# Griffin-style block on one core: the second tile's token roots reach rows by way of DRAM instead of TensorE

## The chip, the cores and the metric

The kernel runs on one core of a Trainium2 chip. The metric is the device time of one execution in microseconds (us), as the median of three timed runs. Beside these runs one execution was recorded by the hardware profiler; all rows of a profile below come from that one.

The engines are named as the profile names them: PE is TensorE with its matmuls, PEld its weight loads, DVE is VectorE, ACT is ScalarE, POOL is GpSimd and SP is SyncE. POOL and SP issue most DMAs here, each into a queue of its own; both queues run on the same 16 DMA engines.

## The reference

One layer over 2048 tokens of width 1024, in float32. The part that bears on this change is the first norm, whose inverse root per token scales all that follows:

```python
def rms_norm(x, g):
    xf = x.astype(jnp.float32)
    y = xf * lax.rsqrt(jnp.mean(xf * xf, axis=-1, keepdims=True) + EPS)
    return (y * g.astype(jnp.float32)).astype(x.dtype)

def hybrid_layer(x, norm_g, w_in, ...):
    h = rms_norm(x, norm_g)
    u = jnp.einsum('bsd,dc->bsc', h, w_in)
    v_c, b_c, c_c, z_c, q, k, v, z_a, gate_logits = jnp.split(u, SPLIT_POINTS, axis=-1)
    y_c = b_c * causal_depthwise_conv(c_c * v_c, conv_w) * jax.nn.silu(z_c)
    y_a = jnp.einsum('bsc,cd->bsd', y_c, w_conv_out)
    q, k = rms_norm(heads(q), q_norm_g), rms_norm(heads(k), k_norm_g)
    o = sliding_window_attention(q, k, heads(v), sinks) * jax.nn.silu(z_a)
    y_b = jnp.einsum('bsc,cd->bsd', o, w_attn_out)
    g_a, g_b = jnp.split(jax.nn.sigmoid(gate_logits + gate_b), N_BRANCHES, axis=-1)
    return x + jnp.einsum('bsd,de->bse', g_a * y_a + g_b * y_b, w_out)
```

(`heads` stands for the reshape into heads of 64. The attention looks back over 128 positions.)

## The kernel before

**Tiling.** The tokens are worked in two tiles of 1024 (`T`), called t = 0 and t = 1. Within a tile, q is the half of 512 tokens (`H`). Activations stand with channels on the 128 rows (partitions) and tokens along them, so that PE can take them as the moving operand. Each matmul in float32 is made of three in the fast 32-bit form, from a high and a low part of each operand, and the products of a 2 x 2 block of outputs are made in seven parts instead of eight, from sums of operands (`sunit`, L493; its products run in line L480). A unit like `cv0` or `z1` is one such block. `SEQ0` and `SEQ1` give the units of the two tiles in order.

**What sets the order.** The order is written out by hand and not by a scheduler. PE runs through the units; after each product, `run` goes on by one tick, prepares a piece of the next weights, calls the functions that `put(n, f)` has set down for that tick, and lets DVE do some steps of woven chains. So everything that is not a product hangs on a tick number, and each engine and each DMA queue takes its instructions in the order in which they were called.

**The attention** of tile t runs inside the same units, in 32 pieces (head group j, block b). A piece `3_7` has these steps: scores on PE (L1027), exponentials on ACT, a turn of 32 x 32 blocks on DVE, a way out to DRAM and back (`fd`, then `x`, both on POOL's queue: L1071, L1078), copies `xh` and `yp` on ACT, the low part `xl` on DVE, four selects on POOL (L1099), then the values matmuls `po` on PE (L1116), whose result goes to DRAM by a write on SP and an adding write `od` on POOL (L1132).

**The roots of tile 1.** The sum of squares of a token is taken with tokens on the rows, so the root of each token stands on its row: a column of 128 values for each block of 128 tokens. While tile 0's gate units run, `h_stats` loads the eight blocks of tile 1 (`x_0` to `x_7`, on POOL's queue, L1372), squares them on ACT, makes the inverse roots on DVE in small steps on 128 x 2 (`x_rsqrt`, `hr`), and keeps them in `rt[q]`, one tile of 128 x 4 for each half q.

To scale activations that have channels on the rows, the 512 roots of a half must stand along each row, the same in all 128 rows. That is done by `h_prep`, which starts with unit `z0` of tile 0: `roots(q)` calls `x_roots`, which has PE turn each root column, spread over 128 columns, into a bank (four matmuls against `ident` for each half, L614, in two banks `ptr` that are borrowed from the attention's scores), and has ACT copy the bank to `rb[q]` (L616).

Then, for four pairs of channel chunks j, `ld` loads `h` (L1418, POOL's queue, four loads for each j), `norm` scales it on DVE by `rb[q]` and writes three of four to DRAM (`hd`, L1425), and sums of the four are written as well (`sdh`). The first pair follows three ticks into `z0`, right behind the roots, the others at ticks 15, 28 and 80 (`H_AT`). In tile 0 the roots are turned by the same `x_roots`; this stays.

**Names in the z units.** `Xz`, `Vz` and `Y` are the three banks of a unit; `wz_...` are its weights in high, low and sum forms; `zin` is what is gated and `zs` the gate. `Vz<-s5z,Y` is an add on DVE that reads `Y` before PE goes on to write it. `th` is the same kind of step in a gate unit.

**Slots.** Tiles of 128 x 512 come from one pool of 19 slots (`slot`), and a tile whose slot was in use waits for those who used it.

Of the kernel before, what the change touches and what calls it, by code (L numbers as in the profile page):

```python
# [8 lines left out]
F32 = mybir.dt.float32  # L9
# [6 lines left out]
P = 128  # L16
# [3 lines left out]
H = 512  # L20
HB = H // P
NB = T // P
# [83 lines left out]
def block_kernel(  # L106
# [12 lines left out]
    nc = tc.nc  # L119
    S = x.shape[1]  # L120
    NT = S // T
# [12 lines left out]
    ps_s = ctx.enter_context(tc.tile_pool(name="ps_s", bufs=1, space=bass.MemoryType.PSUM))  # L134
    ps_m = ctx.enter_context(tc.tile_pool(name="ps_m", bufs=3, space=bass.MemoryType.PSUM))
    dram = ctx.enter_context(tc.tile_pool(name="dram", bufs=1, space=bass.MemoryType.DRAM))

    def slot(shape, dt, name):
        return big.tile(shape, dt, tag="big", name=name)
# [7 lines left out]
    def mbank(name):  # L147
        return ps_m.tile([P, HB, P], F32, tag="m", name=name)
# [14 lines left out]
    ocd = [dram.tile([KC, P, T], F32, name=f"ocd{t}") for t in range(NT)]  # L163
    ycd = [dram.tile([KC, P, T], F32, name=f"ycd{t}") for t in range(NT)]
    hd = [None] + [dram.tile([KC, P, T], F32, name=f"hd{t}") for t in range(1, NT)]
    sd = {}
    for key in [(k, t) for t in range(NT) for k in "hca"][1:] + [("w", 0)]:
        sd[key] = dram.tile([4, KP, P, H], F32, name="sd" + "_".join(str(i) for i in key))
# [4 lines left out]
    def hs(q):  # L173
        return slice(q * H, (q + 1) * H)
# [426 lines left out]
    def x_square(xt, ss, i, junk=None):  # L601

        nc.scalar.activation(out=xt if junk is None else junk, in_=xt, func=AF.Square, accum_out=ss[:, i : i + 1])

    def x_rsqrt(t, b0, n, ss, dst, root=False):
        ms = small.tile([P, n], F32, tag="sm", name=f"ms{t}_{b0}")
        return rsqrt(ms, n, f"hr{t}_{b0}", ss, 1.0 / D, lambda r: nc.vector.tensor_copy(dst, r), root)

    def x_roots(t, q, rs, pt=None):

        if pt is None:
            pt = mbank(f"ptr{t}_{q}")
        for b in range(HB):
            nc.tensor.transpose(pt[:, b, :], rs[:, b : b + 1].to_broadcast([P, P]), ident)  # L614
        rb = slot([P, H], F32, f"rb{t}_{q}")
        nc.scalar.copy(rb, pt.rearrange("p b q -> p (b q)"))  # L616
        return rb
# [4 lines left out]
    def x_norm(h, c, rb):  # L622
        vec.scalar_tensor_tensor(
            out=h, in0=h, scalar=gain(c), in1=rb, op0=ALU.mult, op1=ALU.mult)
# [53 lines left out]
    def put(n, f):  # L678
        at.setdefault(max(n, tick[0] + 1), []).append(f)
# [524 lines left out]
    def sums_of(key, j, r, eng, n0=None):  # L1204

        def first():
            sub(r[0, 0], r[0, 1], r[0, 0])
            eng.dma_start(sd[key][0, j], r[0, 0])
            sub(r[0, 1], r[1, 1], r[0, 1])
            eng.dma_start(sd[key][2, j], r[0, 1])  # L1210

        def second():
            sub(r[1, 1], r[1, 1], r[0, 0])
            eng.dma_start(sd[key][1, j], r[1, 1])
            sub(r[1, 0], r[1, 0], r[1, 1])
            eng.dma_start(sd[key][3, j], r[1, 0])

        if n0 is not None:
            put(n0, first)
            put(n0 + 1, second)  # L1220
        return second, first
# [142 lines left out]
    def h_stats(t, n0):  # L1364

        st = x_state(t)
        xs, rt, seen_ = st["x"], {}, {}

        def ld(b):
            xs[b] = upool.tile([P, 2 * H + 2], F32, tag="u", name=f"x{t}_{b}")[:, 0:D]  # L1370
            r0 = t * T + b * P
            nc.gpsimd.dma_start(xs[b], x2[r0 : r0 + P, :])  # L1372

        def square(b):
            if b % 2 == 0:
                st["ss"][b] = small.tile([P, 2], F32, tag="sx", bufs=3, name=f"ss{t}_{b}")
            x_square(xs[b], st["ss"][b - b % 2], b % 2)

        def norm(b0):
            q, i = divmod(b0, HB)  # L1380
            if i == 0:
                rt[q] = small.tile([P, HB], F32, tag="sr", bufs=2, name=f"rt{t}_{q}")
            seen_[b0] = x_rsqrt(t, b0, 2, st["ss"][b0], rt[q][:, i : i + 2])

        for b in range(NB):
            put(n0 + 2 * b, lambda b=b: ld(b))
            put(n0 + 2 * b + 3, lambda b=b: square(b))
            if b % 2:
                put(n0 + 2 * b + 4, lambda b=b: norm(b - 1))
                put(n0 + 2 * b + 6, lambda b=b: seen_[b - 1]())  # L1390
        st["rt"] = rt

    def h_prep(t, n0):

        st = x_state(t)
        rb = {}

        def roots(q):
            if q == 0:
                rb["banks"] = ps_s.tile([P, 2, HB, P], F32, tag="s", name=f"ptr{t}")  # L1400
            rb[q] = x_roots(t, q, st["rt"][q], rb["banks"][:, q])

        for q in range(2):
            put(n0 + H_AT[0] + q, lambda q=q: roots(q))
        for j in range(KP):
            r = {}

            def ld(q, j=j, r=r):
                if j < H_UP and q == 0:
                    for p in range(2):  # L1410
                        two = upool.tile([P, 2 * H + 2], F32, tag="u", name=f"h{t}_{2 * j + p}")
                        for k in range(2):
                            r[p, k] = two[:, hs(k)]
                for p in range(2):
                    if j >= H_UP:
                        r[p, q] = slot([P, H], F32, f"h{t}_{q}_{2 * j + p}")
                    c = 2 * j + p
                    nc.gpsimd.dma_start(  # L1418
                        r[p, q], xt2[c * P : (c + 1) * P, t * T + q * H : t * T + (q + 1) * H])

            def norm(q, j=j, r=r):
                for p in range(2):
                    x_norm(r[p, q], 2 * j + p, rb[q])
                    if (p, q) != (0, 1):
                        nc.gpsimd.dma_start(hd[t][2 * j + p, :, hs(q)], r[p, q])  # L1425

            n = n0 + 1 + H_AT[j]
            for q in range(2):
                put(n + q, lambda q=q, f=ld: f(q))
                put(n + q + 3, lambda q=q, f=norm: f(q))  # L1430
            sums_of(("h", t), j, r, nc.gpsimd, n + 7)
# [35 lines left out]
    for n in range(S // P // 2):  # L1467
        t, c0 = divmod(2 * n * P, T)
# [7 lines left out]
    def x_state(t):  # L1476
        return state.setdefault(t, {"raw": {}, "ops": {}, "x": {}, "ss": {}})
# [3 lines left out]
    st = x_state(0)  # L1481
# [177 lines left out]
    for t in range(NT):  # L1659
# [29 lines left out]
        if t + 1 < NT:  # L1689
            h_stats(t + 1, tick[0] + STATS_AT)  # L1690
# [76 lines left out]
```

## Time and profile before

| | us |
|---|---|
| median of three runs | 1890.16 |
| lowest and highest of them | 1889.24, 1890.19 |
| the profiled execution | 1888.86 |
| its span, first to last instruction | 1887.1 |

| where it is | from the span's start, us |
|---|---|
| `rt` written by DVE (four copies) | 420.9 to 463.5 |
| `ptr` turned on PE, tile 1 | 575.0 to 578.5 |
| `h` scaled on DVE (sixteen steps) | 589.0 to 807.9 |

How to read the profile: a row of a timeline gives the start, the duration, the engine, the line of the kernel, the operation, its output and inputs by the program's names without buffer numbers, shapes, and a count where equal instructions follow one another. Square brackets at its end give how long the engine had stood idle before and what it waited for. Rows of waits give who waited for whom, the total, the number of times and the longest. A row of windows gives the stretch, the busy time of PE, PEld, DVE, ACT and POOL with instruction counts, the granted clock of PE, the share of time that the DMA engines were busy, and the GB/s they moved. The granted clock of PE is 1.000 over the whole run.

### The profile page before, as it was taken

What the parts mean: (1) busy time and instruction counts of PE and PEld (TensorE: products, weight loads), DVE (VectorE), ACT (ScalarE), POOL (GpSimd) and SP (SyncE); (2) the same over time, 40 slices, a digit from 0 to 9 for tenths busy, and PEclk for the clock granted to TensorE, in tenths of its full rate; (3) what the DMA queues carried; (4) which work ended last, traced back from release to release, by engine and by line L of the source; (5) the groups of instructions that cost most, each with busy time, mean ns of one, the idle gap of its engine ahead of it and who ended that gap; (6) DMA issues with size and microseconds to landing.
All of it is one profiled execution on the core that took longest, in us unless ns stands there. A gap on an engine that the chain in (4) does not pass through costs nothing.

```text
span 1887.1 us, 27889 instructions
## 1 busy us (share of the span) xinstructions
PE 1879.4 (100%) x8638; PEld 1565.4 (83%) x8638; DVE 1539.9 (82%) x2536; ACT 989.2 (52%) x1993; POOL 728.3 (39%) x1038
## 2 busy tenths in 40 slices
PE   9999999999999999999999999999999999999999
PEld 7888888888888888888887888888888888888887
DVE  7989888789878889887579988988888779887654
ACT  7665554567665345435455645556566436344321
POOL 1472454556767111021075445656666211121000
PEclk9999999999999999999999999999999999999999
DMA  8475566689989978899367667768888869999653
GB/s 307 130 212 174 141 176 191 182 252 294 253 244 261 319 272 296 290 288 290 112 186 219 183 169 206 208 166 238 248 237 259 269 244 342 321 281 274 222 173 110
DMA packets 261188, 435.81 MB, mean 231 GB/s; under 512 B 33648, under 2 KB 124784, under 8 KB 261040
## 3 DMA queue, kind: packets, MB, share of 16 engines
q1 hardware_dynamic: 202848, 314.13, 50.6%
q0 software_dynamic: 58048, 119.87, 24.2%
q8 instruction: 69, 1.13, 0.3%
q14 instruction: 79, 0.65, 0.1%
q10 hardware_dynamic: 144, 0.03, 0.0%
HBM read 279.48 MB, written 154.42 MB: 230 GB/s over the span
## 4 chain that ended last, share of the span: by engine, by line
PE 84%; issue 5%; DVE 5%; DMA 3%; POOL 1%; ACT 1%; SPq 0%; POOLq 0%; DVEq 0%; ACTq 0%
PE Y L480 30%; PE Vcv L480 5%; PE Xcv L480 5%; PE s L1027 3%; PE Xz L480 2%; PE Xb L480 2%; PE Vb L480 2%; PE Vz L480 2%; PE Xza L480 2%; PE Xo L480 2%; PE Vo L480 2%; PE Vza L480 2%; PE po L1116 2%; PE Vyb L480 2%; PE Xyb L480 2%
## 5 line engine op out<-in xcount | busy, mean ns | idle before, releaser
L1078 POOL DMA_DIRECT2D x<-fd x256 | 144.2, 612 | 73.1 <-DMA fd<-f 42.9
L1099 POOL TENSOR_SCALAR_AFFINE_SELECT xh<-xh 64x512 fp32r<-64x512 f32 x64 | 67.4, 1053 | 130.2 <-DVE xl L262 95.7
L1051 ACT ACTIVATE p<-s,st,rq 128x128 f32<-128x128 f32 x256 | 113.1, 451 | 7.4 <-DMA lows<-kd 3.3
L1071 POOL DMA_DIRECT2D fd<-f x64 | 39.2, 613 | 176.3 <-DVE f L262 156.8
L480 PE MATMUL Xcv<-oph,wcv_ah 128*128 128x512 f32 x256 | 79.1, 390 | 0.0
L1132 POOL DMA_DIRECT2D od<-o x64 | 69.4, 1091 | 24.1 <-DMA od<-o 9.1
L855 POOL DMA_DIRECT2D q2d<-q_h x64 | 44.4, 693 | 82.7 <-ACT q_h L850 81.7
L1322 POOL DMA_DIRECT2D md<-thyb x32 | 27.5, 874 | 101.7 <-DVE thyb L262 88.8
L1099 POOL TENSOR_SCALAR_AFFINE_SELECT xl<-xl 64x512 fp32r<-64x512 f32 x64 | 62.5, 976 | 4.4
L1099 POOL TENSOR_SCALAR_AFFINE_SELECT yp<-xl 64x512 fp32r<-64x512 f32 x64 | 56.6, 885 | 3.1
L1099 POOL TENSOR_SCALAR_AFFINE_SELECT yp<-yp 64x512 fp32r<-64x512 f32 x64 | 54.8, 856 | 4.2
L480 PEld LDWEIGHTS Xcv<-oph,wcv_ah 128*128 128x128 f32 x256 | 47.6, 188 | 9.4
L262 DVE SCALAR_TENSOR_TENSOR y<-u,cols,y 128x512 f32<-128x512 f32 x64 | 51.5, 805 | 3.7 <-ACT y L1161 2.5
L262 DVE TENSOR_TENSOR opa<-ina,opa 128x512 fp32r<-128x512 f32 x56 | 36.2, 687 | 18.8 <-ACT opa L297 18.8
L262 DVE TENSOR_TENSOR p<-p,st 128x512 f32<-128x512 f32 x64 | 49.2, 769 | 2.8
L1051 ACT ACTIVATION_READ_ACCUMULATOR p<-s,st,rq 128x1 f32 x256 | 50.8, 198 | 0.0
L362 ACT CAST wcv_sh<-wcv_raw 128x1024 fp32r<-128x1024 f32 x16 | 16.9, 1054 | 63.9 <-DVE wcv_raw L262 63.9
L480 PE MATMUL Xcv<-oph,wcv_al 128*128 128x512 f32 x128 | 49.9, 390 | 0.0
L855 POOL DMA_DIRECT2D q2d<-q_l x64 | 44.2, 691 | 14.2 <-DVE q_l L262 10.0
L262 DVE TENSOR_TENSOR opc<-inc,opc 128x512 fp32r<-128x512 f32 x56 | 36.1, 686 | 14.4 <-ACT opc L297 14.2
L262 DVE STREAM_TRANSPOSE f<-p 128x512 f32<-128x512 f32 x64 | 45.4, 710 | 2.6 <-DVE p L262 0.2
L480 PE MATMUL Y<-oph,wcv_d 128*128 128x512 f32 x192 | 46.4, 390 | 0.0
(793 smaller groups left out, 6596.6 us busy)
## 6 DMA issues: line engine op xcount, KB each, us to landing
wcv_raw<-in_w_in SPq DMA_DIRECT2D x32, 512.0 KB, 4.1
q<-q2d SPq DMA_DIRECT2D x64, 256.0 KB, 4.7
v<-vd SPq DMA_DIRECT2D x128, 128.0 KB, 4.4
fd<-f POOLq DMA_DIRECT2D x64, 256.0 KB, 3.8
x<-fd POOLq DMA_DIRECT2D x256, 64.0 KB, 3.4
gd<-th SPq DMA_DIRECT2D x64, 256.0 KB, 3.5
wq_raw<-in_w_in SPq DMA_DIRECT2D x16, 512.0 KB, 5.1
q2d<-q_h POOLq DMA_DIRECT2D x64, 128.0 KB, 3.8
```

Of the source, the lines that this page charges most:

```text
L262: r = f(*args, **kw)
L362: return (lambda: nc.scalar.copy(hi, src), lambda: vec.tensor_tensor(out=lo, in0=src, in1=hi.bitcast(F32), op=ALU.subtract))
L480: nc.tensor.matmul(ps, lhsT=w[:, j, :], rhs=b[:, m, :], start=start and j == 0 and i == 0, stop=j == KP - 1 and i == 2, skip_group_check=n ...
L855: nc.gpsimd.dma_start(q2d[t][j][half, q * 2 * HB : (q + 1) * 2 * HB, i, e, :], src[HALVES[e]].bitcast(F32).rearrange("p (b x) -> p b x", x ...
L1027: nc.tensor.matmul(to, lhsT=w, rhs=x_, start=n == 0, stop=n == 2, skip_group_check=h == 1)
L1051: nc.scalar.activation(out=p[:, i, :], in_=sg[:, i, HD : 3 * HD], func=AF.Exp, bias=st[:, 1, i : i + 1], scale=rv[:, i // 2, i % 2 : i % 2 ...
L1071: nc.gpsimd.dma_start(fd, f)
L1078: nc.gpsimd.dma_start(x[QUADS[k]], src[k])
L1099: nc.gpsimd.affine_select(out=d4, in_=s4, pattern=[[0, 2], [-32 * sg, 2], [0, G], [-sg, 32]], compare_op=ALU.is_gt if prev else ALU.is_ge, ...
L1116: nc.tensor.matmul(po[:, cs], lhsT=v2[:, kind, :], rhs=xx[:, :, h * HD : (h + 1) * HD], start=h == 0 and n == 0, stop=n == 2, skip_group_c ...
L1132: put(tick[0] + ADD_WAIT, lambda: nc.gpsimd.dma_start(to, o[UH].rearrange("p c e q -> p (c e) q"), accum_op=ALU.add))
L1322: nc.gpsimd.dma_start(md[t][k, :, hs(q)], m, accum_op=ALU.add)
```

## The change

The roots of tile 1 take another way from `rt[q]` to `rb[q]`. `h_stats` writes each half's 128 x 4 roots to a DRAM buffer `rxd`, in the order block, token, so that 512 roots stand in a row; `roots(q)` in `h_prep` then loads that row into all 128 rows of `rb[q]`. Both DMAs are issued on POOL. The turns on PE, the bank pair `ptr` and ACT's two copies are no longer called for tile 1. Nothing else is edited.

```diff
     hd = [None] + [dram.tile([KC, P, T], F32, name=f"hd{t}") for t in range(1, NT)]
+    rxd = [None] + [dram.tile([NB, P], F32, name=f"rxd{t}") for t in range(1, NT)]
...
                 put(n0 + 2 * b + 6, lambda b=b: seen_[b - 1]())
-        st["rt"] = rt
+        for q in range(2):
+            put(n0 + 2 * (q + 1) * HB + 6, lambda q=q: nc.gpsimd.dma_start(
+                rxd[t][q * HB : (q + 1) * HB].rearrange("b r -> r b"), rt[q]))
...
         def roots(q):
-            if q == 0:
-                rb["banks"] = ps_s.tile([P, 2, HB, P], F32, tag="s", name=f"ptr{t}")
-            rb[q] = x_roots(t, q, st["rt"][q], rb["banks"][:, q])
+            rb[q] = slot([P, H], F32, f"rb{t}_{q}")
+            src = rxd[t][q * HB : (q + 1) * HB].rearrange("b r -> (b r)")
+            nc.gpsimd.dma_start(rb[q], src.unsqueeze(0).to_broadcast([P, H]))
```

How the instructions stand. The numbers at the end of names are the program's buffer numbers, which shift by a few from one kernel to the other, as line numbers do.

PE, around the second four turns, between the products 1 and 7 of unit `z0`, before:

```order
L480 MATMUL Xz_0_6198<-oph_2_3_533,wz_0_ah 128x512 x2
L480 MATMUL Xz_0_6198<-oph_2_3_533,wz_0_al 128x512
L614 MATMUL ptr_6284<-ident,rt_1_4717 128x128 x4
L480 MATMUL Y<-oph_7_0_910,wz_0_th 128x512 x2
L480 MATMUL Y<-oph_7_0_910,wz_0_tl 128x512
```

and now:

```order
L481 MATMUL Xz_0_6201<-oph_2_3_534,wz_0_ah 128x512 x2
L481 MATMUL Xz_0_6201<-oph_2_3_534,wz_0_al 128x512
L481 MATMUL Y<-oph_7_0_911,wz_0_th 128x512 x2
L481 MATMUL Y<-oph_7_0_911,wz_0_tl 128x512
L481 MATMUL Y<-oph_7_1_848,wz_0_th 128x512 x2
```

The four turns are gone, and so are the other four, which stood ahead of this product; the rest of PE's list is the same.

POOL, at the end of the loads of `x_0` to `x_7`, before:

```order
L1078 DMA x_2_2_4667<-fd_2_2_4581 32x4x128 x4
L1071 DMA fd_2_3_4707<-f_2_3_4705 128x512
L1372 DMA x_7_4721<-in_x 128x1024
L1132 DMA od_104<-o_1_7_4569 64x4x128
L1099 AFFINE_SELECT xh_2_1_4697<-xh_2_1_4697 64x512
```

and now:

```order
L1373 DMA x_7_4722<-in_x 128x1024
L1393 DMA rxd_111<-rt_0_4384 128x4x1
L1133 DMA od_104<-o_1_7_4570 64x4x128
L1100 AFFINE_SELECT xh_2_1_4698<-xh_2_1_4698 64x512
L1100 AFFINE_SELECT yp_2_1_4700<-yp_2_1_4700 64x512
L1100 AFFINE_SELECT yp_2_1_4700<-xl_2_1_4699 64x512
L1100 AFFINE_SELECT xl_2_1_4699<-xl_2_1_4699 64x512
```

The write of the first half's roots stands ahead of the od add and of the selects of piece `2_1`. The second write stands behind the selects of piece `2_3`, ahead of the od add of `2_1` and the loads of `x_2_5`.

POOL, in unit `z0`, where the first `h` loads stand, before:

```order
L1099 AFFINE_SELECT xl_3_5_6243<-xl_3_5_6243 64x512
L1132 DMA od_104<-o_3_3_6171 64x4x128
L1078 DMA x_3_7_6317<-fd_3_7_6252 32x4x128 x4
L1418 DMA h_0_6329<-in_xt 128x512
L1418 DMA h_1_6330<-in_xt 128x512
```

and now:

```order
L1100 AFFINE_SELECT xl_3_5_6246<-xl_3_5_6246 64x512
L1404 DMA rb_0_6287<-rxd_111 128x512
L1133 DMA od_104<-o_3_3_6174 64x4x128
L1079 DMA x_3_7_6315<-fd_3_7_6255 32x4x128 x4
L1404 DMA rb_1_6321<-rxd_111 128x512
L1421 DMA h_0_6323<-in_xt 128x512
L1421 DMA h_1_6324<-in_xt 128x512
```

Both loads of `rb` stand ahead of the first load of `h`, with the od add and the four loads of `x_3_7` between them. DVE's list, which scales `h` by `rb`, and SP's list are the same in both kernels.

## The prediction, made before the changed kernel ran

> **What bounds the kernel now.** I read the head of the profile's page first, then who TensorE (PE) waited for, and then the timeline of each engine around the three places that the change touches.
>
> ```profile
> span 1887.1 us, 27889 instructions
> PE 1879.4 (100%) x8638; PEld 1565.4 (83%) x8638; DVE 1539.9 (82%) x2536; ACT 989.2 (52%) x1993; POOL 728.3 (39%) x1038
> PE Y L1496 <- DVE zero L181: 1.5, 1, 1.5
> ...
> PE Vya L480 <- ACT zas L1282: 0.2, 1, 0.2
> ```
>
> PE is busy for all but 7.7 us of the span. The view of its waits has seven rows, of which the first and the last stand above, and they come to 3.9 us. So a microsecond taken from PE's list of instructions is a microsecond of the whole, and a microsecond by which another engine is late for PE is lost for good. The sum therefore has two kinds of terms: what leaves PE's list, and where a later operand newly makes PE wait.
>
> The profiled execution took 1888.86 us, 1.76 above its span. The median of the three timed runs is 1890.16, 1.30 above the profiled one. I make the sum against the profiled execution and add 1.30 at the end. About 0.2%, 3.8 us, is what a measurement of this kernel can tell from no change.
>
> **Part 1: the eight turns on PE go.** The rows are PE's timeline (start, duration), first around the turns (L614), then the same stretch of the next z unit, which has no turns in it.
>
> ```profile
> 575.02 0.60 PE L614 MATMUL ptr<-ident,rt 128*128 128x128 f32 x4
> 575.37 0.70 PE L480 MATMUL Xz<-oph,wz_ah 128*128 128x512 f32 x2
> ...
> 578.20 0.60 PE L614 MATMUL ptr<-ident,rt 128*128 128x128 f32 x4
> 578.56 0.71 PE L480 MATMUL Y<-oph,wz_th 128*128 128x512 f32 x2
> ...
> 581.39 0.61 PE L480 MATMUL Vz<-oph,wz_th 128*128 128x512 f32 x2
> ...
> 596.44 0.63 PE L480 MATMUL Xz<-oph,wz_ah 128*128 128x512 f32 x2
> ...
> 599.19 0.61 PE L480 MATMUL Y<-oph,wz_th 128*128 128x512 f32 x2
> ```
>
> The durations overlap, so I use distances between starts. Four turns and the twelve matmuls behind them take 578.20 - 575.02 = 3.18 us; twelve such matmuls without turns take 599.19 - 596.44 = 2.75. The second group takes 581.39 - 578.20 = 3.19. The turns cost 0.43 + 0.44, and I take **0.9 us** off PE. That is all this part can bring: PE did not wait for the roots, which DVE had finished 575.0 - 463.5 = 111 us earlier.
>
> ```profile
> L607 DVE COPY rt<-hr_r x4: 161/173/332, 420.9 to 463.5; 128x2 f32<-128x2 f32 x4
> ```
>
> ScalarE (ACT) loses two copies of the turned roots (L616). This I cost at nothing, because the next ACT step there waits for PE in any case:
>
> ```profile
> 575.65 0.59 ACT L616 COPY rb<-ptr 128x512 f32<-128x512 f32 x1 [1.04 <-PE ptr L614]
> ...
> 578.40 0.60 ACT L1282 ACTIVATE zs<-Xz 128x512 f32<-128x512 f32 x1 [0.86 <-PE Xz L480]
> ```
>
> The score bank that ptr borrowed is next written in the second tile's attention, far down PE's list, so its earlier release brings nothing. Some tiles of the z units get other slots of the ring. What they follow is freed by the same values matmuls and od adds as before; I cost this at nothing too, and a late one would show as a new wait of ACT for a slot.
>
> **Part 2: two writes of roots on GpSimd (POOL).** The first one enters POOL's list between the load of x_7 and the od add. Behind it stand the four selects whose result PE takes in the values matmuls po_2_1.
>
> ```profile
> L855 POOL DMA_DIRECT2D q2d<-q_h x64: 689/689/751, 61.8 to 1059.5; - x64
> L921 POOL DMA_DIRECT2D rkd<-k_rt x8: 484/487/520, 952.7 to 956.1; - x8
> ...
> 445.68 1.12 POOL L1132 DMA_DIRECT2D od<-o  x1
> 446.37 1.20 POOL L1099 TENSOR_SCALAR_AFFINE_SELECT xh<-xh 64x512 fp32r<-64x512 f32 x1
> ...
> 449.22 0.76 POOL L1099 TENSOR_SCALAR_AFFINE_SELECT xl<-xl 64x512 fp32r<-64x512 f32 x1
> ...
> 450.93 0.28 PE L1116 MATMUL po<-xl,v 128*128 128x256 f32 x1
> ...
> 445.67 0.15 DVE L291 TENSOR_TENSOR hr_t<-hr_r 128x2 f32<-128x2 f32 x1
> ...
> 446.46 1.11 DVE L293 SCALAR_TENSOR_TENSOR hr_r<-hr_t,hr_r 128x2 f32<-128x2 f32 x1
> ...
> PEld Y L480 <- DVE th L262: 0.3, 1, 0.3
> ```
>
> The write has 128 x 4 = 512 pieces of 4 bytes. The trace has none like it. The q2d write has 64 x 8 = 512 pieces too, of 256 bytes, and holds POOL 0.69 us; a write of roots of K with 16 pieces holds it 0.49. I take 0.69, the row with the same count; bounds are 0.49 and, below, 4.0. The selects then end at 449.98 + 0.69 = 450.67, and PE wants the last of them at 450.93: slack is 0.95, so po_2_1 is just in time.
>
> VectorE (DVE) has no slack there. Its 128x2 steps, 0.15 us where no select runs, last until the select beside them ends (446.46 + 1.11 is the end of the select that began at 446.37), and PE already waits 0.3 for DVE's th. Selects that start 0.69 later meet other DVE steps. I give this 0.3 us of new PE wait, between 0 (the overlaps only move) and 0.7 (the whole shift).
>
> The second write comes behind the selects of unit 2_3, ahead of an od add and the loads of x_2_5:
>
> ```profile
> 472.76 2.34 POOL L1078 DMA_DIRECT2D x<-fd  x4 [0.64 <-DMA fd<-f]
> ...
> x<-fd POOLq DMA_DIRECT2D x4, 64.0 KB, 3.9
> ...
> 483.70 0.62 ACT L1085 CAST xh<-x 128x512 fp32r<-128x512 f32 x1
> ```
>
> The last of these lands near 474.5 + 3.9 = 478.4, and ACT takes it at 483.70. Some 5 us of cover hide this write. If it held the queue longer than that, ACT would stop.
>
> **Part 3: two loads of rows on POOL ahead of the h loads.** This is the largest term. POOL's rows, then the landing of the first h load (the last number), then DVE, POOL and PE behind it:
>
> ```profile
> 580.01 1.03 POOL L1132 DMA_DIRECT2D od<-o  x1
> 580.80 2.45 POOL L1078 DMA_DIRECT2D x<-fd  x4
> 582.99 1.92 POOL L1418 DMA_DIRECT2D h<-in_xt  x3
> ...
> h<-in_xt POOLq DMA_DIRECT2D x1, 256.0 KB, 6.0
> ...
> 589.00 2.06 DVE L262 SCALAR_TENSOR_TENSOR h<-h,cols,rb 128x512 f32<-128x512 f32 x2 [1.25 <-DMA h<-in_xt]
> ...
> 597.12 0.69 DVE L262 TENSOR_TENSOR Vz<-s5z,Y 128x512 f32<-128x512 f32 x1
> 597.72 0.68 DVE L262 TENSOR_TENSOR xl<-x,xh 128x512 fp32r<-128x512 f32 x1
> ...
> 602.49 1.09 POOL L1099 TENSOR_SCALAR_AFFINE_SELECT xl<-xl 64x512 fp32r<-64x512 f32 x1
> ...
> 604.86 0.28 PE L1116 MATMUL po<-xl,v 128*128 128x256 f32 x1
> ...
> 608.53 1.23 DVE L262 TENSOR_TENSOR wz_sl<-wz_raw,wz_sh 128x1024 fp32r<-128x1024 f32 x1 [0.39 <-ACT wz_sh L362]
> ...
> 580.00:590.00 10.00, 10.00 (x48) 8.39 (x47) 7.26 (x11) 6.04 (x11) 7.51 (x13) 1.00 0.88 219
> ```
>
> The h load issued at 582.99 lands 6.0 us later, and DVE has waited 1.25 us for it when it starts at 589.00. So DVE's order hangs on that load alone. Both new loads stand ahead of it in POOL's list. One costs POOL what an x piece or an h load does, (582.99 - 580.80) / 4 = 0.55 or 1.92 / 3 = 0.64: together 1.2 us. They also bring 512 KB into a queue whose window moves 219 GB/s with 0.88 of its engines' time used: 2.4 us if all of it lies ahead of h, nothing if it slips into gaps. The first is issued some 4 us ahead of h and has that long to drain, the second just ahead of it, so I take 0.9. The h load comes **2.1 us** later (1.2 to 3.6), and DVE with it.
>
> The roots themselves are not late: the first load starts near 580.1 and, with the 6.0 of the h load, is there by 586.
>
> Behind the h step the first idle time of DVE is the 0.39 at 608.53: the Vz add and the last xl move by the same 2.1. POOL's selects of unit 3_7 follow xl; they end at 602.49 + 1.09 = 603.58, and PE takes them at 604.86. Slack 1.28. The Vz add ends at 597.81, and PE overwrites Y at 599.19: slack 1.38, the same answer. In the changed kernel PE is also 0.9 ahead. PE would newly wait 2.1 + 0.9 - 1.28 = **1.7 us**.
>
> **The sum**: -0.9 + 0.3 + 1.7 = **+1.1 us**. That is 1889.96 for a profiled execution, and with the 1.30 above, **1891.3** for the median.
>
> **Rivals.**
>
> *The queue absorbs it.* A load of K's rows, the same kind as the new ones, lands in 3.0 us, so about half of h's 6.0 may be time in the queue.
>
> ```profile
> L932 POOL DMA_DIRECT2D k_r<-rkd x8: 518/522/563, 962.1 to 966.8; - x8
> ...
> DMA to landing us min/median/max: 2.8/3.0/4.1
> ```
>
> If h, issued 1.2 later, waits 1.2 less there, and the 512 KB go into the gaps, h is on time. PE then keeps its 0.9, the overlaps of part 2 give nothing, and the median is 1889.3. For it: 12% of the engines' time is free in that window. Against it: the second load is issued just ahead of h, in the same queue. Chance 30%.
>
> *The 4-byte pieces hold POOL.* The mechanism: pieces go out one by one as packets, and POOL cannot run ahead of them. Price: the page's queue row.
>
> ```profile
> q0 software_dynamic: 58048, 119.87, 24.2%
> ```
>
> One packet takes 0.242 x 16 x 1887.1 / 58048 = 0.126 us of one engine, so 512 on 16 engines take 4.0 us. If POOL stood for that time, po_2_1 would be 4.0 - 0.95 = 3.05 late instead of in time; the sum becomes +4.1, and the median 1894.3, slower by 0.22%. It decides once a write holds POOL over 3.7 us. Against it is the q2d row: with an equal count its median is its least, 0.69. Chance 8%.
>
> The Trainium skill, in "DMA: Bandwidth & Descriptors", section "Rules for kernel authors", speaks against this write: a strided last dimension becomes one descriptor per element, and it says a plain copy with a rearranged pattern is 19 times slower than the hardware's transpose. Taking 19 times the q2d row as an estimate, a write would hold 13 us and the median come near 1903; no run here shows a 4-byte piece, and the q2d row shows that the count alone does not do it.
>
> **How the numbers follow.** The forecast, h late by more than the slack, has 60%: from -0.9 + 0 + 0.8 = -0.1 (h 1.2 late; 1890.1) to -0.9 + 0.7 + 3.2 = +3.0 (h 3.6 late; 1893.2). With the 30% of the first rival, down to 1889.3 and 0.4 less for the scatter of the median, the range is 1888.9 to 1893.2. The 8% of the second rival lies above it, and 2% is left for a gain that I do not see. Faster by over 0.2% would need 3.8 us, and PE sheds 0.9: 2%. Slower: 8%. Within: 90%.
>
> **What would show it.** Of part 1: no L614 row near 575, and twelve Xz matmuls in 2.75 us behind po. Of part 2: the rxd writes hold POOL near 0.69 and the wait of PE for th grows from 0.3. Of part 3: DVE's wait for h grows from 1.25 to about 3.3, and new PE rows wait for xl or Vz near 600 to 605. I am wrong if DVE waits for rb instead of h, if PE waits at po_2_1, or if no new PE wait shows at all.

## The result and the profile after

| | before | after |
|---|---|---|
| median, us (six runs each, side by side) | 1889.80 | 1901.45 |
| lowest and highest, us | 1889.24, 1892.95 | 1897.65, 1904.26 |
| profiled execution, us | 1888.86 | 1903.55 |
| its span, us | 1887.1 | 1901.8 |

The ratio is 1.0059, with a 95% interval of 1.0046 to 1.0073: the change costs 11.65 us, where +1.1 was forecast.

First the head of the page, after the change:

```profile
span 1901.8 us, 27883 instructions
PE 1883.7 (99%) x8630; PEld 1568.4 (82%) x8630; DVE 1539.2 (81%) x2536; ACT 988.9 (52%) x1991; POOL 729.2 (38%) x1042
```

and the view of PE's waits (who waited for what, the total, times, longest):

```profile
PE s L1028 <- DMA v<-vd: 7.6, 1, 7.6
PE Y L481 <- DVE Vz L263: 1.8, 1, 1.8
PE Y L1499 <- DVE zero L182: 1.5, 1, 1.5
PE Y L481 <- DVE yap L263: 1.4, 1, 1.4
```

PE does eight matmuls less, and yet its busy time grew by 4.3 us: some matmuls ran slower. Two long rows of waits are new, 7.6 and 1.8 us.

To place the loss I compare the starts of the same `po` matmuls in both profiled executions. The difference is -0.21 us at `po_2_1`, +10.81 at `po_2_2` (the first write of roots stands between them), +9.91 at `po_3_5` (the eight turns are gone), +13.65 at `po_3_7` (the first `h` step), +14.69 at the start of tile 1 and at the end. So there are two places of loss, 11.0 and 3.7 us, one of gain between them, 0.9, and a last microsecond, of which 0.8 is PE's wait for `yap` (0.6 before, 1.4 now). Below, the first place of loss (the writes) is called the first site and the second one (the loads ahead of `h`) the third site, since the turns lie between them.

**The first site.** Windows of before (stretch, its length, busy time of PE, PEld, DVE, ACT and POOL, granted clock, DMA share, GB/s):

```profile
450.00:455.00 5.00, 4.87 (x26) 4.03 (x25) 4.76 (x13) 4.21 (x13) 2.60 (x5) 1.00 0.97 290
455.00:460.00 5.00, 5.00 (x25) 4.18 (x25) 4.74 (x12) 4.83 (x9) 2.35 (x4) 1.00 0.97 232
```

The same windows of after, 5 us behind the write:

```profile
450.00:455.00 5.00, 4.38 (x21) 3.21 (x19) 4.79 (x11) 1.97 (x9) 2.63 (x5) 1.00 1.50 181
455.00:460.00 5.00, 0.00 (x0) 0.00 (x0) 0.60 (x1) 2.54 (x4) 0.00 (x0) 0.83 0.99 82
460.00:465.00 5.00, 2.56 (x9) 2.39 (x10) 3.85 (x10) 4.03 (x8) 2.21 (x3) 0.50 0.74 208
```

The two last numbers tell it. The DMA engines count as fully busy (the view's share can pass 1; I read it only as full), but they move 82 GB/s where they moved 232. Everything in flight arrives late. From the view of DMA issues (count, KB each, median us to landing), those issued from 446 to 456, after:

```profile
gd<-th SPq DMA_DIRECT2D x1, 256.0 KB, 12.8
...
x<-fd POOLq DMA_DIRECT2D x4, 64.0 KB, 11.4
lows<-kd SPq DMA_DIRECT2D x2, 64.0 KB, 15.1
```

The same three in the same stretch before (the first and the last with two issues):

```profile
gd<-th SPq DMA_DIRECT2D x2, 256.0 KB, 3.9
...
x<-fd POOLq DMA_DIRECT2D x4, 64.0 KB, 3.5
...
lows<-kd SPq DMA_DIRECT2D x2, 64.0 KB, 7.0
```

Both queues are hit, SP's as well as POOL's. The trace's records of single packets show the same. The write itself goes out as 16 data packets of 128 bytes, each of which took 0.04 us. Of the packets that began from 452 to 453, in its wake, 22 took over 1 us, on both queues, the longest 4.82 us; before, the longest in that microsecond took 0.31. The timelines of POOL, ACT and PE in after show who pays (start, duration; idle time before and its cause in brackets):

```profile
445.36 0.78 POOL L1393 DMA_DIRECT2D rxd<-rt  x1
...
449.65 0.76 POOL L1100 TENSOR_SCALAR_AFFINE_SELECT xl<-xl 64x512 fp32r<-64x512 f32 x1
...
457.46 1.06 ACT L604 ACTIVATE x<-x 128x1024 f32<-128x1024 f32 x1 [4.86 <-DMA x<-in_x]
...
462.44 0.66 PE L1028 MATMUL s<-lows,kq 128*128 128x384 f32 x1 [7.56 <-DMA v<-vd]
462.90 1.00 PE L1028 MATMUL s<-kq,q 128*128 128x192 f32 x4
463.70 0.57 PE L1028 MATMUL s<-lows,kq 128*128 128x384 f32 x1
464.07 1.05 PE L481 MATMUL Xga<-oph,wga_ah 128*128 128x512 f32 x2
...
468.89 0.63 PE L481 MATMUL Vga<-oph,wga_sh 128*128 128x512 f32 x2
```

POOL held the write for 0.78 us and went on; its selects end at 450.41, in time. The loss is not on POOL. PE stops for 7.56 us ahead of the scores. The row puts this down to a load of `v`, but what came last for PE is an operand of the scores: by the trace the second load of `lows`, on SP's queue, landed at 462.31, 0.13 us before PE started. Two runs below have the same distance, e1 (461.61 and 461.74) and e13 (457.24 and 457.38); in e13, whose row names `v` too, the loads of `v` landed only after PE had started. ACT's wait of 4.86 us for `x_7` is another sign of the same hold-up.

After that stop PE's granted clock is 0.50: twelve matmuls take 468.89 - 464.07 = 4.82 us instead of the 2.75 of the prediction's rows, 2.07 more, and the scores from 462.44 to 464.07 take 1.63 where a run below with the clock at 1.00 has 0.87. Ahead of the stop PE also waits longer for `th`: from the start of `po_2_1` to that of the next products it is 1.38 us (450.49 to 451.87), where it was 1.00 (450.70 to 451.70). So 7.56 + 2.07 + 0.76 + 0.38 = 10.8 of the 11.0 us.

**The third site**, in after: POOL's loads ahead of `h`, DVE's wait for `h`, and PE.

```profile
591.20 0.58 POOL L1404 DMA_DIRECT2D rb<-rxd  x1
...
594.66 1.01 POOL L1404 DMA_DIRECT2D rb<-rxd  x1
595.22 2.60 POOL L1421 DMA_DIRECT2D h<-in_xt  x4
...
603.17 1.65 DVE L263 SCALAR_TENSOR_TENSOR h<-h,cols,rb 128x512 f32<-128x512 f32 x2 [5.18 <-DMA h<-in_xt]
...
611.07 0.73 PE L481 MATMUL Y<-oph,wz_th 128*128 128x512 f32 x2 [1.81 <-DVE Vz L263]
...
615.52 0.63 PE L481 MATMUL Vz<-oph,wz_th 128*128 128x512 f32 x2
```

and the window in which most of these matmuls lie, in after:

```profile
612.00:616.00 4.00, 4.00 (x13) 3.12 (x12) 3.97 (x4) 0.00 (x0) 3.82 (x4) 0.59 1.00 348
```

DVE waits 5.18 us for `h` (1.25 before), and PE 1.81 us for the `Vz` add behind it. The clock then falls again, to 0.59 in the window: twelve matmuls take 615.52 - 611.07 = 4.45 us. Of the 3.7 us, 1.81 are the wait and some 1.6 the clock (a run below has 2.85 for these twelve).

### The profile page after: what moved, and what is told of

Read it like the earlier page. It is cut to its first block, busy times and chain, and to the rows that moved or that the text cites. A ratio compares the mean times of both kernels' runs of the same rounds, so it can differ in the third digit from the quotient of the medians.

```text
span 1901.8 us, 27883 instructions
## 1 busy us (share of the span) xinstructions
PE 1883.7 (99%) x8630; PEld 1568.4 (82%) x8630; DVE 1539.2 (81%) x2536; ACT 988.9 (52%) x1991; POOL 729.2 (38%) x1042
## 4 chain that ended last, share of the span: by engine, by line
PE 90%; DMA 4%; POOL 3%; issue 1%; DVE 1%; ACT 1%; SPq 0%; POOLq 0%; DVEq 0%; ACTq 0%
PE Y L481 30%; PE Vcv L481 5%; PE Xcv L481 5%; PE s L1028 3%; PE Xga L481 2%; PE Xb L481 2%; PE Vb L481 2%; PE Vo L481 2%; PE Xo L481 2%; PE Xyb L481 2%; PE Vyb L481 2%; PE Xza L481 2%; PE Vza L481 2%; PE Vga L481 2%; PE po L1117 2%; PE kv L570 2%
## 5 line engine op out<-in xcount | busy, mean ns | idle before, releaser
L1028 PE MATMUL s<-lows,kq 128*128 128x384 f32 (+2 forms) x128 | 44.3, 346 | 7.6 <-DMA v<-vd 7.6
```

The costliest lines, as they stand in the source:

```text
L1028: nc.tensor.matmul(to, lhsT=w, rhs=x_, start=n == 0, stop=n == 2, skip_group_check=h == 1)
```

## The experiments

All medians are compared with runs of the kernel before on the same chip, whose medians were 1889.65, 1889.90, 1890.12, 1890.25 and 1890.24 us in the five groups. "Writes only" means that PE still turns the roots, and the writes to DRAM are merely added.

### Is it the writes, and what about them?

Writes alone (e1):

```diff
+        st["rt"] = rt
...
-            rb[q] = slot([P, H], F32, f"rb{t}_{q}")
-            src = rxd[t][q * HB : (q + 1) * HB].rearrange("b r -> (b r)")
-            nc.gpsimd.dma_start(rb[q], src.unsqueeze(0).to_broadcast([P, H]))
+            if q == 0:
+                rb["banks"] = ps_s.tile([P, 2, HB, P], F32, tag="s", name=f"ptr{t}")
+            rb[q] = x_roots(t, q, st["rt"][q], rb["banks"][:, q])
```

> The two writes of roots alone: the turns on PE stay and rxd is not read. Theory (the 512 pieces of 4 bytes clog the DMA engines that all queues share): po_2_2 starts 9 to 13 us later than the 463.55 of before, PE waits 6 to 9 us at the scores behind unit gb, and the time is 1899 to 1903. Rival (the loss of the change comes with the two loads of rows ahead of h): po_2_2 within 0.5 us of before, time 1889 to 1891.

1899.0 us, ratio 1.0052 (1.0029 to 1.0075), `po_2_2` 10.2 us late. PE's wait in e1:

```profile
PE s L1028 <- DMA lows<-kd: 6.9, 1, 6.9
```

and the window of e1 around it:

```profile
455.00:460.00 5.00, 0.00 (x0) 0.00 (x0) 0.60 (x1) 1.15 (x3) 0.00 (x0) 0.77 0.68 57
```

The same hole, without a read of what was written. Two writes of 2 KB each cost over 9 us.

The loads as in the change, but each half written as 128 pieces of 16 bytes, in the order in which the roots lie (e2):

```diff
-                rxd[t][q * HB : (q + 1) * HB].rearrange("b r -> r b"), rt[q]))
+                rxd[t][q * HB : (q + 1) * HB].rearrange("b r -> (b r)").rearrange(
+                    "(r b) -> r b", b=HB), rt[q]))
```

> The change with the write in another layout: each row of rt goes out as one piece of 16 bytes, 128 pieces in place of 512 of 4 bytes, at the same tick; the loads are the same. The kernel leaves out the reordering of the roots by token, so the second tile is scaled by roots of other tokens. Theory (4-byte pieces): po_2_2 within 0.7 us of before, DVE still waits 4 to 5 us for h near 600, the time is 1892 to 1894.5. Rival (any DMA put at that place between the load of x_7 and the od add is enough): po_2_2 9 to 13 us later as in the changed kernel, time 1899 to 1903.

1891.39 us, ratio 1.0008 (0.9997 to 1.0019): the big loss is gone. `po_2_2` is 1.9 late (PE waits 1.4 us ahead of the scores), the third site costs 1.3.

512 pieces of 4 bytes again, writes only, but each into a row of 512 bytes of its own (e3), and 512 pieces of 64 bytes side by side (e4, whose pieces are 16 columns of `ident`; only e3's edit is shown):

```diff
-    rxd = [None] + [dram.tile([NB, P], F32, name=f"rxd{t}") for t in range(1, NT)]
+    rxd = [None] + [dram.tile([NB, P, P], F32, name=f"rxd{t}") for t in range(1, NT)]
...
-                rxd[t][q * HB : (q + 1) * HB].rearrange("b r -> r b"), rt[q]))
+                rxd[t][q * HB : (q + 1) * HB, :, 0].rearrange("b r -> r b"), rt[q]))
```

> Writes only, as in e1, but each 4-byte piece goes to a 512-byte row of its own. If it is neighbours that share a line in DRAM: no clog, po_2_2 within 1 us of before, time 1889 to 1891. If it is the small piece as such or the count of 512: as e1, 1899 to 1903.

> Writes only, 512 pieces as in e1, but of 64 bytes each (taken from ident, not the roots). If the count of pieces makes the clog: as e1, po_2_2 9 to 13 us later, time 1899 to 1903. If it is the 4 bytes, by size or by neighbours that share a line: po_2_2 within 1.5 us of before, time 1889 to 1892.

1889.67 us, ratio 1.0000 (0.9989 to 1.0011), and 1889.52, ratio 1.0001 (0.9990 to 1.0012). In e3:

```profile
455.00:460.00 5.00, 5.00 (x25) 4.14 (x24) 4.75 (x13) 4.46 (x9) 2.84 (x4) 1.00 0.99 261
```

Same count, same 4 bytes, no hole. The profile page's line on POOL's queue (packets, MB, share of 16 engines' time), in e1 and then in e3:

```profile
q0 software_dynamic: 58112, 119.87, 24.1%
q0 software_dynamic: 58112, 119.87, 24.0%
```

Against the 58048 packets of before, two writes are 64 packets in both, and the page of the profile has 58112 also for the runs below with 16 and with 64 pieces (e15, e16). So the pieces do not go out as a packet each. Neither the count nor the size of the pieces makes the hole, but that small pieces fall close together in DRAM. (In e4's profiled run `po_2_2` is 1.2 us late; its median shows no loss.)

### How close, and how many?

Writes only, with the row of a piece cut from 512 bytes to 64 (e5), 32 (e11), 16 (e12) and 8 (e13); only the last size of the DRAM tile differs from e3 (16, 8, 4, 2 in place of `P`).

> Only the two writes are added, as 512 pieces of 4 bytes again, each into a row of 64 bytes of its own (before, 512 bytes gave 1889.67 us, and neighbouring 4-byte pieces 1899.0). Theory: pieces hold each other up where they fall into one line of DRAM, and the line is 64 bytes or less: 1889.7 us within 1 us, po_2_2 within 1 us of the kernel before, the landing of the first write near 7.5 us. Rival: what they share is larger than 64 bytes (up to 512): then some of the loss is back, 1892 to 1899 us, and po_2_2 is 3 to 10 us late.

> Only the two writes, 512 pieces of 4 bytes each, one piece in every 32 bytes, so that two pieces fall into each 64 bytes of DRAM. Theory (pieces that fall into the same 64 bytes hold each other up, and one in 64 bytes cost nothing): a small part of the loss is back, po_2_2 0 to 3 us late, 1889.5 to 1892.5 us. Rival (what they share is 32 bytes or less): as one in 64 bytes, 1889.9 us within 0.7 us, po_2_2 within 0.7 us.

> Only the two writes, one 4-byte piece in every 16 bytes, four to each 64 bytes of DRAM. Theory (the hold-up grows with the number of pieces that share): between two to a line and the change's sixteen: po_2_2 1 to 7 us late, 1890.5 to 1896 us. Rival (it needs pieces that touch each other): as one in 64 bytes, 1889.9 us within 0.7 us.

> Only the two writes, 512 pieces of 4 bytes each, one in every 8 bytes, eight to each 64 bytes of DRAM; no two touch. Theory (the number of pieces that fall into the same 64 bytes sets the hold-up): between four to 64 bytes (po_2_2 2.0 us late, 1890.5 us) and the change's sixteen (10 us, 1899.0 us): po_2_2 3 to 8 us late, 1891.5 to 1897 us. Rival (only pieces that touch hold each other up): as four to 64 bytes or less, po_2_2 at most 2 us late, 1889.5 to 1891 us.

Then the neighbouring form with fewer pieces: one block of the four (e14, 128 pieces), half a block (e16, 64) and 16 tokens (e15).

```diff
-                rxd[t][q * HB : (q + 1) * HB].rearrange("b r -> r b"), rt[q]))
+                rxd[t][q * HB : q * HB + 1].rearrange("b r -> r b"), rt[q][:, 0:1]))
```

> Only the two writes, in the change's neighbouring 4-byte form, but of one block of tokens each instead of four: 128 pieces, sixteen to each 64 bytes. Theory (the time that the pieces hold each other up is summed over them): a quarter of the hold-up, which is shorter than what PE has in stock: po_2_2 at most 2 us late, 1889.5 to 1891.5 us, the write's landing between the 7.5 us of pieces apart and 9 us. Rival (one crowded 64 bytes holds the queues whatever the number of pieces): po_2_2 6 to 11 us late, 1896 to 1900 us.

> Only the two writes, each of just 16 pieces of 4 bytes that touch: the first 16 tokens of one block, one stretch of 64 bytes. Theory (the hold-up is summed over the pieces that fall into one row of 512 bytes, and rows are served beside each other; the 128 pieces of one row took some 5 us more to land than pieces apart): an eighth of that, 0.6 us: the second write lands in 3 to 4.5 us, po_2_2 at most 1.5 us late, 1889.5 to 1891 us. Rival (it goes by 64 bytes: 16 pieces in one of them take the whole 5 us, and the stretches of 64 bytes are served beside each other): the second write lands in 7.5 to 9.5 us, and 1894 us or more.

> Only the two writes, each of 64 pieces of 4 bytes that touch: half a block, 256 bytes. Theory (summed over the pieces of one row of 512 bytes): half of the 5 us: the second write lands in 5 to 6.5 us, as eight pieces in each 64 bytes did (5.9 us, which are 64 in 512 bytes), po_2_2 1.5 to 4.5 us late, 1890.5 to 1893.5 us. Rival (it goes by 64 bytes): the second write lands in 7.5 to 9.5 us, and 1894 us or more.

| run | pieces of 4 B in a write | in each 64 B | landing of the second write, us | `po_2_2` late, us | median, us | ratio (95%) |
|---|---|---|---|---|---|---|
| e3 | 512 | one in 512 B | 3.1 | -0.2 | 1889.67 | 1.0000 (0.9989 to 1.0011) |
| e5 | 512 | 1 | 3.2 | 0.4 | 1890.11 | 1.0000 (0.9991 to 1.0009) |
| e11 | 512 | 2 | 3.0 | 0.6 | 1890.36 | 1.0000 (0.9991 to 1.0010) |
| e12 | 512 | 4 | 4.5 | 2.0 | 1890.51 | 1.0005 (0.9995 to 1.0014) |
| e13 | 512 | 8 | 5.9 | 2.9 | 1891.81 | 1.0006 (0.9997 to 1.0016) |
| e1 | 512 | 16 | 9.4 | 10.2 | 1899.00 | 1.0052 (1.0029 to 1.0075) |
| e14 | 128 | 16 | 8.0 | 8.4 | 1897.13 | 1.0033 (1.0022 to 1.0045) |
| e16 | 64 | 16 | 7.5 | 7.3 | 1895.57 | 1.0027 (1.0016 to 1.0037) |
| e15 | 16 | 16 | 4.4 | 0.4 | 1890.43 | 1.0001 (0.9991 to 1.0010) |

The landing tells the runs apart better than the medians, whose intervals hold 1 in e12 and e13; it is of one execution each. The rows are of this kind, here the second writes of e3, e1, e13 and e14:

```profile
rxd<-rt POOLq DMA_DIRECT2D x1, 2.0 KB, 3.1
rxd<-rt POOLq DMA_DIRECT2D x1, 2.0 KB, 9.4
rxd<-rt POOLq DMA_DIRECT2D x1, 2.0 KB, 5.9
rxd<-rt POOLq DMA_DIRECT2D x1, 0.5 KB, 8.0
```

It is the first write that makes `po_2_2` late. That one enters a fuller queue and lands in 7.5 us in e3, 7.7 in e5, 8.3 in e11, 9.1 in e12, 10.5 in e13, 12.7 in e14, 13.2 in e16 and 8.6 in e15; for e1 the trace has no landing of it.

One or two pieces in 64 bytes land like pieces far apart. From four on the landing grows with the crowding, although in e12 and e13 no two pieces touch. So crowding does it, not touching. e11's rival (nothing is shared beyond 32 bytes) still stands, and fits rather better: the loss starts where two pieces share 32 bytes (e12), not where two share 64 (e11).

My sum over pieces fell. A quarter of the pieces (e14) costs nearly as much as all of them, not a quarter; half of that again (e16) hardly less; and the 16 pieces of one stretch (e15) cost 1.3 us of landing (4.4 against 3.1), neither an eighth of the 5 us nor the whole. The hold-up grows with the crowding, and with the number of pieces steeply up to 64 and slowly beyond. **Over what stretch, or which engines, it is summed stays open**; so does whether 64 bytes is the chip's own measure.

PE's loss isn't proportional to the landing either. Of the first write, 3.0 us more than in e3 (e13) make PE 2.9 late, 5.7 more (e16) 7.3, and 5.2 more (e14) 8.4. In e13 the clock stayed at 1.00 behind PE's wait of 2.28 us; in e16 and e14 PE waited 4.9 and 5.7 us (the latter in two waits, the longer 5.2) and slow matmuls came on top, with the granted clock of the whole run at 0.998. PE's timeline in e13:

```profile
457.38 0.41 PE L1028 MATMUL s<-lows,kq 128*128 128x384 f32 x1 [2.28 <-DMA v<-vd]
...
458.25 0.63 PE L481 MATMUL Xga<-oph,wga_ah 128*128 128x512 f32 x2
458.71 0.39 PE L481 MATMUL Xga<-oph,wga_al 128*128 128x512 f32 x1
```

### Why only the first of the two writes costs

In e1 the first write makes `po_2_2` 10.2 late, and everything after it adds 1.2. First theory: it costs because `x_7`'s load stands right by it. Writes only, the first four ticks later (e8):

```diff
-            put(n0 + 2 * (q + 1) * HB + 6, lambda q=q: nc.gpsimd.dma_start(
+            put(n0 + 2 * (q + 1) * HB + 6 + 4 * (1 - q), lambda q=q: nc.gpsimd.dma_start(
```

> Only the two writes are added, in their neighbouring 4-byte form, but the first goes out four ticks (some 17 us) later, where no load of x stands behind it in POOL's queue. Theory: a write always holds all other transfers for 5 to 8 us, and what it costs depends on whether a load that is needed soon stands behind it; without x_7's load behind it, ACT isn't held and PE doesn't run dry: 1889.7 to 1892 us, with the DMA share still above 1.3 at under 180 GB/s for some 4 us after the write. Rival: supplies are short everywhere, so that the clog costs the same at any tick: 1897 to 1900 us, with a PE wait of 6 us or more some 5 us behind the write.

1900.9 us, ratio 1.0051 (1.0037 to 1.0065): the theory fell. The first write, now at 458.55, costs PE nothing, but the second, 16 us behind it, makes PE 8.8 us later. (The profiled run, 1898.05 us, was the fastest of four.) Windows of e8:

```profile
462.00:466.00 4.00, 4.00 (x22) 3.43 (x21) 3.83 (x10) 3.95 (x13) 2.69 (x5) 1.00 1.15 75
...
478.00:482.00 4.00, 0.01 (x1) 0.00 (x0) 3.03 (x5) 3.95 (x8) 1.82 (x4) 0.88 1.65 18
```

Both clog (75 and 18 GB/s); one is hidden. Second theory: what was loaded ahead covers about one clog, and a hidden one uses it up. So the second write alone, at the change's tick (e9: `for q in range(1, 2)`):

> Only the second of the two writes, in its neighbouring 4-byte form, at the change's tick. In the change it cost next to nothing, behind a first write that stopped PE for 10 us; with the first write put four ticks later, it was the first that cost nothing and the second 9 us. Theory: a write costs what is missing from the stock of loads and fragments ahead of PE; a stop of PE fills the stock and a hidden write empties it. Alone at its tick it finds the stock of the kernel before: some part of 9 us at most, 1889.5 to 1895 us, and under the 9 us that it cost behind a hidden write. Rival: the place alone decides; the tick of the second write has no cover, and it costs its 9 us: 1897 to 1900 us.

1890.51 us, ratio 1.0006 (0.9997 to 1.0015). The clog is there and PE runs through it, in e9:

```profile
475.00:479.00 4.00, 4.00 (x22) 3.42 (x21) 3.93 (x7) 3.95 (x8) 1.11 (x3) 1.00 1.06 70
```

Its tick alone doesn't decide: the second write costs nothing here and 8.8 us behind a hidden one. One of the ten runs of e9 took 1896.74, so the cover may be thin. The stock itself wasn't measured, and that PE's stop refills it, so that the second write of e1 costs little, is argued and not shown.

### The loads, and a version without the crowded writes

VectorE turns the roots in 32 x 32 blocks, each root column repeated eight times, so that a write is 16 pieces of 128 bytes (e6); then the same with the loads two ticks earlier (e7); and the change itself with only the loads moved (e10).

```diff
+        def spread(q):
+            rr = small.tile([P, 32], F32, tag="sm", name=f"rr{t}_{q}")
+            vec.transpose(out=rr, in_=rt[q].unsqueeze(2).to_broadcast([P, HB, 8]))
+            nc.gpsimd.dma_start(
+                rxd[t][q * HB : (q + 1) * HB].rearrange("b (g r) -> g b r", r=32),
+                rr.rearrange("(m k) r -> m k r", k=8)[:, 0])
...
-            put(n0 + 2 * (q + 1) * HB + 6, lambda q=q: nc.gpsimd.dma_start(
-                rxd[t][q * HB : (q + 1) * HB].rearrange("b r -> r b"), rt[q]))
+            put(n0 + 2 * (q + 1) * HB + 6, lambda q=q: spread(q))
...
-            put(n0 + H_AT[0] + q, lambda q=q: roots(q))
+            put(n0 + H_AT[0] + q - 2, lambda q=q: roots(q))
```

(e6 has the first part, e10 the second, e7 both.)

> The change, but VectorE turns the roots in blocks of 32x32 before each write, so that a write is 16 pieces of 128 bytes instead of 512 of 4. The output is the reference's. Theory: the writes now clog nothing; what is left is the eight PE turns' 0.9 us gained, against the two loads that make h late, which cost 1.3 us with the flat write and 3.7 us in the change: 1890 to 1892.5 us, po_2_2 within 1 us of before, h still late at the third site. Rival: it is the way by DRAM as such (write, then two loads of 256 KB each) that clogs: above 1895 us.

> As the run before (VectorE turns the roots, 16 pieces of 128 bytes), but the two loads of rb go out two ticks earlier, so that they no longer stand right ahead of h's loads. The output is the reference's. Theory: the loads cost time only by making h late on POOL's queue; earlier they cost nothing, and the 0.9 us of the PE turns shows: 1888.8 us within 0.7 us, PE's wait for Vz below 0.8 us at the third site. Rival: their 512 KB, or their issue on POOL, hold something else wherever they stand: as the run before, 1890 to 1892.5 us, with a PE wait of 1 us or more at the new place.

> The change with one edit: the two loads of rb go out two ticks earlier. The output is the reference's. Theory: the 3.7 us of the change's third site come from h's loads standing behind the two loads of rb on POOL, as the 1.5 us did with the turned roots: the change's 1901.45 us less 3 to 4 us, 1897.5 to 1898.5 us. Rival: the third site is late because the clogged writes moved the phases of the queues, whatever stands ahead of h: 1900.5 to 1902 us.

| run | median, us | ratio (95%) | lost at the third site, us |
|---|---|---|---|
| e6 | 1891.16 | 1.0003 (0.9994 to 1.0012) | 1.5 |
| e7 | 1888.68 | 0.9991 (0.9982 to 1.0000) | 0.0 |
| e10 | 1896.06 | 1.0034 (1.0022 to 1.0046) | 0.0 |

("Lost" is the shift of `po` from `3_5` to `3_7`, 604.63 - 584.11 = 20.52 us in the kernel before.) PE and DVE in e6:

```profile
601.22 0.73 PE L481 MATMUL Y<-oph,wz_th 128*128 128x512 f32 x2 [1.18 <-DVE Vz L263]
...
604.07 0.62 PE L481 MATMUL Vz<-oph,wz_th 128*128 128x512 f32 x2
...
593.09 0.75 DVE L263 SCALAR_TENSOR_TENSOR h<-h,cols,rb 128x512 f32<-128x512 f32 x1 [4.12 <-DMA h<-in_xt]
...
442.12 0.17 DVE L263 STREAM_TRANSPOSE rr<-rt 128x32 f32<-128x32 f32 x1
```

and DVE in e7:

```profile
589.77 0.75 DVE L263 SCALAR_TENSOR_TENSOR h<-h,cols,rb 128x512 f32<-128x512 f32 x1 [1.63 <-DMA h<-in_xt]
```

With the loads ahead of it `h` comes late and PE waits; with the loads two ticks earlier the wait for `h` is 1.63 us, PE waits nowhere at this site, and the 0.9 us of the turns shows. e10 removes the same 3.7 us from the change. Its median fell by more, 5.4 us against the change's; the profiled runs differ at the first site too (PE stopped 4.4 us instead of 7.56), and I have no cause for it; clogged runs scatter more, 1894.87 to 1899.44 us in e10. e7 beats the change by 12.8 us of median. Against the kernel before it gains 1.2 us, with an interval that ends at no change. Nor is its first site clean: `po_2_2` is 1.2 us late in its profiled run, where PE waits 1.1 for `lows`. In the profiled runs of e6 and e10 PE waits 0.8 us for POOL's selects at `po_2_1`, so there the write's hold of POOL may reach PE; no run separates it.

## Why the prediction was wrong

- **Part 1 was right.** The eight turns took 0.9 us off PE: the shift falls from +10.81 to +9.91 between `po_2_2` and `po_3_5`. The profiled runs of e2, e6, e7 and e10 show the same 0.9. No row of PE's waits in after points at ACT's copies or the slots.
- **Part 2 is the step that failed.** It priced a write by the time that it holds POOL, from the row with the same count of pieces. That hold came out near the price, 0.78 us for 0.69, and `po_2_1` was in time as worked out (in e6 and e10 it was 0.8 late, so the slack was as thin as the sum says). The 0.3 us given for DVE's `th` came out as 0.38. But the term had no place for what the pieces do on the 16 DMA engines, and the q2d row matched the count and not where the pieces fall: its pieces are of 256 bytes, and already 64-byte ones side by side cost nothing (e4). In its place the runs showed 11.0 us at the first site: the transfers of both queues held up, a stop of 7.56 us until SP's loads of `lows` landed, and PE at half clock behind it. e1 shows that the write alone does it, e3 that the same pieces far apart do not.
- **The sentence on the second write was nearly the mechanism.** It said that ACT would stop if the write held the queue longer than the 5 us of cover. The queue was held, and for this write the cover sufficed; for the first write no such sum was made, neither for `x_7` on POOL's queue nor for `lows` on SP's, and there it did not suffice.
- **Part 3 was right in mechanism.** Without the clog (e6) PE waits 1.2 us for the `Vz` add and the site costs 1.5, against 1.7 forecast; in the change `h` came 3.4 us later on top of the shift from the first site (603.17 - 589.00 - 10.81), where 2.1 was forecast within 1.2 to 3.6, and PE waited 1.81. e7 shows that it is the loads' place ahead of `h`. In the change the site cost 3.7 since the half clock came on top; that was not in the sum. e6 as a whole took 1891.16 us, near the forecast of 1891.3, but its profiled run ends 2.5 us later than before's instead of 1.1, so the closeness of the median is no check of each term.
- **The rival "the 4-byte pieces hold POOL" fell as a mechanism**, since POOL held 0.78 us. Its premise fell too: a write is 32 packets in the profile and not 512, so that its 4.0 us of 16 engines lies near the 6.3 us by which the second write of e1 lands later than that of e3 (9.4 against 3.1) by luck. It should have been a rival on the queues, for both POOL's and SP's transfers.
- **The rival "the queue absorbs it"** holds for the 0.9 us alone, and only where the loads go out earlier (e7).
- **The rule of the Trainium skill.** "DMA: Bandwidth & Descriptors" of the Trainium skill, in "Rules for kernel authors", made the write dear through one descriptor per element. The estimate of 1903 from it came near the time, but not through a hold of POOL, so the nearness is luck. That page of the Trainium skill sets its 19 times against the hardware's own transpose, while the estimate set it on a plain write of 256-byte pieces. The trace doesn't bear the count out: e3 and e5 have the same 512 elements and cost nothing. Nearer is what that page of the Trainium skill says in its Specifications, that below 512 bytes the DMA reads, modifies and writes. That would fit pieces that disturb each other in one stretch, but no run here shows that mechanism itself, and by size alone it doesn't tell e1 from e3.
- **The range** left out 1901 because both ends of the write's cost were times of POOL. A transfer without a like row has a second unknown, what it does to the others in flight.

## What to carry to other kernels

Before you spread a column of single elements over DRAM, look where neighbouring pieces fall: 4-byte pieces side by side cost 10 us here for a write of 2 KB, while the same pieces 64 bytes apart, or a 0.17 us turn on VectorE that makes 128-byte pieces, cost nearly nothing. A DMA's price has three parts to be bounded apart: the hold of its issuer, its own landing, and the delay of all other transfers; the third shows as a DMA share near or over 1 at few GB/s. A load that isn't urgent belongs some ticks ahead of an urgent one in a queue, not right before it.

## What the runs showed of the hardware

- Crowded small writes to DRAM hold up the transfers of both queues: 18 to 82 GB/s at a DMA share of 0.68 to 1.65, in windows of 4 and 5 us, where the kernel before moves 232 to 311. Two writes of 64 pieces of 4 bytes (256 bytes each) suffice for a loss of 5.3 us (e16). One write of 512 such pieces is 32 packets, as one of 16 pieces is (e15).
- A wait of PE costs more than its length once the clock falls. After 7.56 us of standstill the granted clock was 0.50 and twelve matmuls took 4.82 us instead of 2.75. How long a wait may be isn't settled: 1.81 us (after, at 611) was followed by 0.59, and 2.28 us (e13) by 1.00. The Trainium skill, in "TensorE: Matmul & The Clock Gate", Part 1, says that the clock is halved after an idle window of some 3.4 us, and that these windows run freely. The slow stretch at the third site, some 611.9 to 615.3, has that length, but PE had been idle for only 1.81 us, so the trace doesn't bear out that it takes a whole idle window.
